# Neighbourhood attention with query blocks shifted by 8 columns and stacked hi/lo operands; the dilated second score over the full array

## Chip, cores and metric

One core of one Trainium2 chip runs the kernel. The metric is device time in microseconds of one execution, the median of the runs; lower is better.

## What is computed

A two-layer encoder over 512 positions of width 1024, batch 1, everything in float32. A layer mixes with 16 heads of 64 (4 differential, 6 dilated, 6 neighbourhood heads), projects the heads back, and applies a gated convolution MLP; both parts are modulated by vectors computed from `c`. What the change touches, cut from the reference:

```python
def neighborhood_attention(q, k, v, rpb):          # grid of 8 rows x 64 columns, position = 64 r + c
    # a query sees all 8 rows and the 16 columns from clip(c - 8, 0, 48)
    s = einsum('bhrqd,bhrjkd->bhrqjk', qg, kr) * (DH ** -0.5) + bias
    s = where(col_mask, s, NEG)
    p = softmax(s.reshape(B, H, rows, 64, 8 * 64))
    return einsum('bhrqn,bhrnd->bhrqd', p, vr)

def dilated_attention(q, k, v):                    # three dilated windows, merged by their log sums
    ...

o = concatenate([o_diff, o_dilated, o_neighbourhood]) @ w_out
x = x + gate * o
```

## The kernel before

**Number format.** A float32 product is made from `fp32r` matmuls: each operand is split into a rounded part (hi) and the rest (lo), and hi·hi, hi·lo and lo·hi are summed in PSUM (`mm3`, L482 to L485). Weights come as float32 from memory on SP's queue (`emit_raw`, L329), ScalarE rounds them (L351) and VectorE or GpSimd subtracts (L353); three or so units of weights are kept ahead.

**Phases.** For each of the two layers: `attention_phase` (projections, then heads), then `ffn_phase`, which begins with `o2`, the part of the output projection that reads the neighbourhood heads, `oT[5]` to `oT[7]`. `o1`, the part that reads the other five chunks, still belongs to `attention_phase`.

**Order of the work in `attention_phase`.** A generator `proj` walks through the projections: V of the differential and dilated heads, Q/K of the dilated pairs, Q/K of neighbourhood pairs 0 and 1 (`qk_na`), V of the neighbourhood heads (L761 to L771), Q/K of pair 2, and, once the dilated heads are done, the split of the first five chunks of the heads' output (L776 to L781) and `o1` (L782 to L788). Beside it runs the list `steps`: 16 differential steps, 24 dilated steps (6 heads x 4 query blocks of 128) and 12 neighbourhood steps (6 heads x 2). Each pass of the loop at L1068 emits about six projection matmuls and, if a step's credit, buffers and keys allow, one step. A step issues its scores at once and its later stages as a chain with lags counted in passes (`Clock.chain`, L278). The framework takes this program order as priority and may put a ready instruction ahead of one that waits. Buffers are counted by hand in `av` (`tmp`, `s`, `pt`, `o`, `ph`, `nat`). In layer 0, `ada_step` (L402) adds one VectorE pass of 1024 columns per modulation column every fourth pass of the loop.

**Dilated step** (`dil_step`, L931). `dil_stack` (L645) has put Khi over Klo on 128 partitions (`ks`) and Qhi twice (`qs`); one full matmul gives Qhi·(Khi + Klo) (L938). The second, L939, multiplies Qlo (tile `ql`) by Khi and uses 64 partitions, those of the head. A VectorE pass adds the mask and takes the extreme (L942), ScalarE takes the exponential and scales (L947, L952), PE transposes P (L813), ScalarE rounds it (L817), VectorE subtracts (L821), and `av_half` multiplies V (whose hi and lo columns stand side by side, so the output has 128 rows) by hi and lo of P (L834, L836). The two halves of the output are then added: a ScalarE copy (L844) and a VectorE addition (L847).

**Neighbourhood step** (`na_step`, L967). `qk_na` (L723) leaves hi and lo of Q and K in column-major order in four tiles `nat`, a head on 64 partitions. A step takes two blocks of 128 queries (16 columns x 8 rows), each with a window of 32 columns (256 keys): three matmuls of 64 partitions per block (L981 to L983). VectorE adds the bias and takes the maximum (L988), ScalarE the exponential (L998), VectorE normalises (L1004), PE transposes four tiles (L1010), ScalarE copies them (L1013), and four float32 products with V (L1027, which the chip runs as eight matmuls of 64 output rows) go into one PSUM tile for two heads. Per pair, ScalarE rounds it (L1035) and VectorE subtracts (L1036) into `oT`. The bias of a head is 384 KB and uses the `ks` buffers (`nab_load`, L962). V of these heads is written to DRAM (L767) and, when the dilated heads are done, loaded in seven windows (`v_na`, L790 to L795).

Of the kernel before, what the change touches and what calls it, by code (L numbers as in the profile page):

```python
# [144 lines left out]
WIN = (0, 8, 24, 32)  # L145


def _na_index():
    idx = np.full((3, 128, 256), -1, np.int64)
    for t, (b, w0) in enumerate(((0, 0), (1, 8), (3, 32))):  # L150
        for q in range(128):
            c, r = 16 * b + q // 8, q % 8
            cs = min(max(c - KW // 2, 0), GW - KW)
            for j in range(256):
                kc, kr = w0 + j // 8, j % 8
                if cs <= kc < cs + KW:
                    idx[t, q, j] = (kr - r + KH - 1) * (2 * KW - 1) + kc - c + KW - 1
    return idx
# [15 lines left out]
def build(ctx, tc, a):  # L174
# [393 lines left out]
    def attention_phase(l, gen, fest):  # L568
# [13 lines left out]
        scr, stk, vs, of, oT, nab, dns = {}, {}, {}, {}, {}, {}, {}  # L582
# [62 lines left out]
        def dil_stack(p):  # L645
# [3 lines left out]
            L = at([128, S], F32R, "ql", 2)  # L649
# [6 lines left out]
            SY.dma_start(Lf[0:64], sv[0, 64:128, 0])  # L656
            SY.dma_start(Lf[64:128], sv[0, 64:128, 1])
# [3 lines left out]
        def v_rows(name, nu, kper, n, done):  # L661
# [11 lines left out]
            for tb, k in seq:  # L673
# [9 lines left out]
                ts = slice(tb * 128, tb * 128 + 128)  # L683
                PE.matmul(outs[tb], h[k][0][:, ts], wh[:, sl], start=(k == 0), stop=False)
                PE.matmul(outs[tb], h[k][0][:, ts], wl[:, sl], start=False, stop=False)
                PE.matmul(outs[tb], h[k][1][:, ts], wh[:, sl], start=False, stop=(k == KD - 1))
# [36 lines left out]
        def qk_na(p):  # L723
            res = []
            for nm, scale in (("cq", 0.125), ("ck", 1.0)):
                b = yield from bank()
                yield from proj_cols((nm, p), h, b)
                while av["nat"] < 2:
                    yield
                av["nat"] -= 2  # L730
                hi = at([128, GW, GR], F32R, "nat", 8)
                lo = at([128, GW, GR], F32R, "nat", 8)
                bv = b.rearrange("p (r c) -> p r c", r=GR)
                hv, lv = hi.rearrange("p c r -> p r c"), lo.rearrange("p c r -> p r c")
                A.activation(out=hv, in_=bv, func=AF.Copy, scale=scale)

                def fin(lv=lv, bv=bv, hv=hv, scale=scale):
                    V.scalar_tensor_tensor(out=lv, in0=bv, scalar=scale, in1=hv.bitcast(F32),
                                           op0=ALU.mult, op1=ALU.subtract)
                    give("pr")  # L740

                ck.after(1, fin)
                res += [hi.rearrange("p c r -> p (c r)"), lo.rearrange("p c r -> p (c r)")]
            stk["c", p] = res
            mark(2, ("c", p))

        def proj():
# [13 lines left out]
            sv = dp.tile([GR, GW, HC * 64], F32, name=f"scv{l}")  # L761
            vt = at([128, 4, HC * 64], F32, "va", 1)

            def done(tb, src, ptag):
                A.copy(vt[:, tb], src)
                give(ptag)
                ck.after(1, lambda: SY.dma_start(sv[2 * tb:2 * tb + 2], vt[:, tb]))  # L767

            yield from v_rows("vc", 4, 2, 384, done)
            ready.add("sv")  # L770
            vs["sv"] = sv  # L771
# [4 lines left out]
            for c in range(5):  # L776
# [4 lines left out]
                oT[c] = (hi, lo)  # L781
            for m in range(KD):  # L782
# [6 lines left out]

        def v_na():  # L790
            vn = at([128, 7, HC * 64], F32, "vb", 1)
            for i in range(7):
                SY.dma_start(vn[:, i], vs["sv"][:, 8 * i:8 * i + 16].rearrange("r c n -> c r n"))
            vs["vc"] = vn
            mark(3, "vc")  # L795
# [32 lines left out]
        def av_half(st, half, vt, hidx, c, hh, fin):  # L828
# [9 lines left out]
            if half == 1:  # L838
                if c not in of:
                    of[c] = at([128, S], F32, "of", 5)  # L840
                t = tmp()
                dst = slice(64 * hh, 64 * hh + 64)
                oth = slice(64 - 64 * hh, 128 - 64 * hh)
                A.copy(t[dst], o[oth])  # L844

                def s1():
                    V.tensor_tensor(out=of[c][dst], in0=o[dst], in1=t[dst], op=ALU.add)  # L847
                    give("o")
                    if fin:
                        fin()  # L850

                ck.after(1, s1)
# [78 lines left out]
        def dil_step(hd, qb, st):  # L931
            p, hh = divmod(hd, 2)
            K, Q, L = stk["b", p]
            lr = slice(64 * hh, 64 * hh + 64)
# [4 lines left out]
            PE.matmul(s, L[lr, sl], K[lr, hh], start=False, stop=True)  # L939
# [22 lines left out]
        def nab_load(hd):  # L962
            b = at([128, 3, 256], F32, "ks", 2)
            SY.dma_start(b, a["nab"][l, hd])
            nab[hd] = b

        def na_step(hd, q2, st):  # L967
            p, hh = divmod(hd, 2)
            qh, ql, kh, kl = stk["c", p]
            hr = slice(64 * hh, 64 * hh + 64)  # L970
            bias = nab[hd]
            vn = vs["vc"]
# [3 lines left out]
            P = take("tmp", (128, 2, 256))  # L976
            for i in range(2):
                qb = 2 * q2 + i
                sl = slice(qb * 128, qb * 128 + 128)
                kw = slice(WIN[qb] * 8, WIN[qb] * 8 + 256)  # L980
# [3 lines left out]
            if hh == 1 and q2 == 1:  # L984
                av["nat"] += 4
            for i in range(2):
                bt = (0, 1, 1, 2)[2 * q2 + i]
                V.tensor_tensor_reduce(out=P[:, i], in0=s[:, i], in1=bias[:, bt], op0=ALU.add, op1=ALU.max,  # L988
                                       scale=1.0, scalar=-3e38, accum_out=mx[:, i:i + 1])
# [4 lines left out]
            box = {}  # L994

            def s1():
                for i in range(2):
                    A.activation(out=P[:, i], in_=P[:, i], func=AF.Exp, bias=mx[:, i:i + 1],  # L998
                                 accum_out=dn[:, i:i + 1])

            def s2():
                V.reciprocal(out=dn, in_=dn)
                for i in range(2):
                    V.tensor_scalar(out=P[:, i], in0=P[:, i], scalar1=dn[:, i:i + 1], scalar2=None, op0=ALU.mult)  # L1004

            def s3():
                pt = take("pt", (128, 2, 2, 128))
                for i in range(2):
                    for kt in range(2):
                        PE.transpose(pt[:, i, kt], P[:, i, kt * 128:kt * 128 + 128], ident)  # L1010
# [4 lines left out]
                box["p"] = ptn  # L1015

            def s4():
                ptn = box["p"]
                if hh == 0 and q2 == 0:
                    of["c", p] = take("o")  # L1020
                o = of["c", p]
                hs = slice(hd * 64, hd * 64 + 64)
                for i in range(2):
                    qb = 2 * q2 + i
                    w = WIN[qb] // 8
                    for kt in range(2):
# [308 lines left out]
```

## Time and profile before

| what | value |
|---|---|
| median of 3 runs | 1386.52 us (1386.37 to 1387.81) |
| profiled execution: span from first to last instruction | 1383.9 us |
| PE, VectorE, ScalarE busy | 1328.0, 896.2, 608.2 us |
| mean granted TensorE clock | 0.990 of 2.4 GHz |
| first layer's dilated scores on PE | 166.8 us on |
| first layer's neighbourhood scores on PE | 250.7 us on |
| last neighbourhood product of layer 1 | starts at 981.5 us |

The profile gives no time of the profiled execution outside its span; what lies around the span is taken as the difference to the median, 2.6 us. In its lines "PE" is TensorE's matmuls, "PEld" its weight loads, "DVE" VectorE, "ACT" ScalarE, "POOL" GpSimd and "SP" the engine whose queue issues most transfers. A matmul's duration contains its passage through the array, so that consecutive matmuls overlap; the cost of one in a stream is the distance between starts. A line of a group gives its count, then busy time in all and mean ns of one, then the idle time before them and what ended it.

### The profile page before, as it was taken

The page shows a single profiled execution, that of the slowest core. Times are in us where ns is not written, and L with a number is a line of the kernel's source. Part 1 is how long each engine was busy: PE and PEld are TensorE (multiplying, and loading weights), DVE is VectorE, ACT ScalarE, POOL GpSimd, SP SyncE. Part 2 cuts the span into 40 slices and gives each one's busy share as a digit, 9 for nine tenths or more (in the row PEclk, how much of TensorE's full clock was granted, in tenths as well). Part 3 has the DMA queues.
Part 4 walks back from the last instruction along what each step waited for, and adds up shares of the span by engine and source line. Part 5 has one row for each costly group of instructions (what it writes and reads, how often), then busy time and mean ns, then how long its engine had stood idle before and what let it go on. Part 6 is the DMA issues. An engine that isn't in the chain of part 4 may idle for free.

```text
span 1383.9 us, 18577 instructions
## 1 busy us (share of the span) xinstructions
PE 1328.0 (96%) x6992; PEld 1109.3 (80%) x6992; DVE 896.2 (65%) x1615; ACT 608.2 (44%) x1051; POOL 177.8 (13%) x116
## 2 busy tenths in 40 slices
PE   5887899999999999999998989999999999999997
PEld 4785678779988888888898867877898888888886
DVE  7968976977776666656675697466576434443443
ACT  3336487645543233223342667775445322332331
POOL 3732321003000000000113232200200000000002
PEclk9999999999999999999999999999999999999998
DMA  9565564644466666665523645142334323333211
GB/s 365 164 182 150 162 208 142 197 134 149 124 195 181 202 180 184 198 196 165 175 76 108 178 140 171 57 126 77 97 98 124 103 94 91 96 102 92 79 44 61
DMA packets 69262, 196.16 MB, mean 142 GB/s; under 512 B 7602, under 2 KB 12850, under 8 KB 69044
## 3 DMA queue, kind: packets, MB, share of 16 engines
q1 hardware_dynamic: 68448, 193.10, 46.3%
q10 hardware_dynamic: 724, 1.87, 0.4%
q8 instruction: 55, 0.90, 0.3%
q14 instruction: 35, 0.29, 0.1%
HBM read 180.78 MB, written 14.16 MB: 141 GB/s over the span
## 4 chain that ended last, share of the span: by engine, by line
PE 85%; DVE 8%; DMA 3%; POOL 2%; issue 1%; ACT 1%; POOLq 0%; SPq 0%; DVEq 0%; ACTq 0%
PE pr L483 12%; PE pr L485 12%; PE pr L484 11%; PE s L484 5%; PE s L485 5%; PE s L483 5%; PE pt L484 4%; PE pt L485 4%; PE pt L483 4%; PE pt L813 2%; PE o L485 2%; PE o L483 2%; PE o L484 2%; PE o L1027 2%; PE s L939 1%
## 5 line engine op out<-in xcount | busy, mean ns | idle before, releaser
L351 ACT CAST whi<-raw 128x1024 fp32r<-128x1024 f32 (+2 forms) x144 | 135.0, 938 | 268.8 <-PE pr L485 103.4
L353 DVE TENSOR_TENSOR wlo<-raw,whi 128x1024 fp32r<-128x1024 f32 (+2 forms) x101 | 111.2, 1101 | 94.9 <-ACT whi L351 94.1
L444 POOL TENSOR_TENSOR tmp<-tmp,tmp 128x256 f32<-128x256 f32 (+1 forms) x38 | 36.7, 966 | 892.5 <-ACT tmp L442 891.2
L351 ACT CAST fhi<-raw 128x1024 fp32r<-128x1024 f32 (+1 forms) x76 | 74.9, 985 | 143.9 <-PE pr L485 53.7
L411 DVE CUSTOM_DVE_ANT_0 tmp<-raw,cb,par 128x1024 bf16<-128x1024 f32 x80 | 106.8, 1336 | 41.6 <-DMA raw<-w_ada 41.5
L485 PE MATMUL pr<-h,whi 128*128 128x512 f32 (+1 forms) x330 | 121.9, 374 | 8.0 <-POOL h L479 7.6
L483 PE MATMUL pr<-h,whi 128*128 128x512 f32 (+1 forms) x330 | 125.9, 382 | 1.6 <-DVE tmp L596 0.7
L353 POOL TENSOR_TENSOR wlo<-raw,whi 128x768 fp32r<-128x768 f32 (+1 forms) x43 | 96.0, 2238 | 243.2 <-ACT whi L351 215.6
L484 PE MATMUL pr<-h,wlo 128*128 128x512 f32 (+1 forms) x330 | 123.1, 373 | 1.0 <-POOL wlo L353 1.0
L353 DVE TENSOR_TENSOR flo<-raw,fhi 128x1024 fp32r<-128x1024 f32 (+1 forms) x76 | 87.4, 1150 | 55.2 <-ACT fhi L351 54.4
L483 PE MATMUL pr<-h,fhi 128*128 128x512 f32 (+1 forms) x244 | 86.7, 357 | 0.0
L484 PE MATMUL pr<-h,flo 128*128 128x512 f32 (+1 forms) x244 | 86.5, 356 | 0.0
L485 PE MATMUL pr<-h,fhi 128*128 128x512 f32 (+1 forms) x244 | 85.5, 357 | 0.5 <-DVE h L479 0.5
L485 PEld LDWEIGHTS pr<-h,whi 128*128 128x128 f32 x330 | 62.1, 190 | 19.8 <-POOL h L479 9.5
L483 PEld LDWEIGHTS pr<-h,whi 128*128 128x128 f32 x330 | 62.7, 190 | 16.0 <-issue 4.1
L484 PEld LDWEIGHTS pr<-h,wlo 128*128 128x128 f32 x330 | 63.1, 191 | 9.7 <-POOL wlo L353 1.2
L1157 ACT ACTIVATE tmp<-tmp 128x512 f32<-128x512 f32 x44 | 27.6, 631 | 94.3 <-DVE tmp L1152 77.4
L821 DVE TENSOR_TENSOR pl<-pt,ph 128x512 fp32r<-128x512 f32 x80 | 54.4, 686 | 14.7 <-ACT ph L817 14.5
L904 DVE TENSOR_REDUCE sm<-s 128x1 f32<-128x512 f32 x64 | 43.0, 682 | 28.4 <-PE s L902 28.0
L813 PE MATMUL pt<-cst,tmp 128*128 128x128 f32 x320 | 48.6, 274 | 13.3 <-DVE tmp L920 11.0
L817 ACT CAST ph<-pt 128x512 fp32r<-128x512 f32 x80 | 46.7, 586 | 32.3 <-PE pt L813 31.2
L477 ACT ACTIVATE h<-tmp,mod,gsc 128x256 fp32r<-128x256 f32 (+1 forms) x58 | 35.3, 621 | 53.3 <-DVE tmp L474 52.5
(265 smaller groups left out, 3657.3 us busy)
## 6 DMA issues: line engine op xcount, KB each, us to landing
raw<-w SPq DMA_DIRECT2D x132, 512.0 KB
raw<-w_ada SPq DMA_DIRECT2D x80, 512.0 KB
raw<-w SPq DMA_DIRECT2D x72, 384.0 KB
araw<-w_ada SPq DMA_DIRECT2D x16, 512.0 KB
raw<-w SPq DMA_DIRECT2D x16, 320.0 KB
ks<-nab SPq DMA_DIRECT2D x12, 384.0 KB
scr0b<-nat SPq DMA_DIRECT2D x12, 256.0 KB
scr1b<-nat SPq DMA_DIRECT2D x12, 256.0 KB
```

What stands on the lines that cost most here:

```text
L351: A.copy(hi, r)
L353: (G if on_pool else V).tensor_tensor(out=lo, in0=r, in1=hi.bitcast(F32), op=ALU.subtract)
L411: V.tensor_tensor_reduce(out=junk, in0=r, in1=cb, op0=ALU.mult, op1=ALU.add, scale=1.0, scalar=par[:, OFF_B + l * 48 + j:OFF_B + l * 48 + ...
L444: self.last = self.eng.tensor_tensor(out=self.sq[0][:, sl], in0=self.sq[0][:, sl], in1=self.sq[m][:, sl], op=ALU.add)
L477: ins = A.activation(out=hi, in_=t, func=AF.Identity, scale=A_col, bias=sh_col)
L483: PE.matmul(out, wh, hh, start=first, stop=False)
L484: PE.matmul(out, wl, hh, start=False, stop=False)
L485: return PE.matmul(out, wh, hl, start=False, stop=last)
L813: PE.transpose(pt[:, kt], P[:, kt * 128:kt * 128 + 128], ident)
L817: A.copy(st["ph", half][:, :, sl], pt)
L821: V.tensor_tensor(out=st["pl", half][:, :, sl], in0=st["pt", qb], in1=st["ph", half][:, :, sl].bitcast(F32), op=ALU.subtract)
L904: V.tensor_reduce(out=nm[:, m:m + 1], in_=s, axis=AX.X, op=ALU.max, negate=True)
```

## The change

The dilated Qlo tile gets 128 rows, Qlo twice, for both heads; the second score becomes Qlo·(Khi + Klo) with 128 partitions. For the neighbourhood heads:

- queries are rotated by 8 columns, so that a block of 128 holds columns 16b - 8 to 16b + 7; the first block holds columns 56 to 63 and 0 to 7. Inner blocks see exactly two tiles of 16 columns (128 keys each), the two halves of the first block one tile each;
- hi and lo of Q and K are stacked on 128 partitions by 12 transfers a pair (`na_stack`), and two full matmuls replace three of 64 partitions;
- V is split into hi and lo, written to DRAM and loaded as four column tiles right after its projection; P is transposed to seven tiles a head, split into hi and lo, and ten `fp32r` matmuls a head give the product, whose halves are added as for the other heads;
- the bias of a head shrinks to 128 x 384 values (192 KB) with buffers of its own.

```diff
-            L = at([128, S], F32R, "ql", 2)
+            L = at([128, 2, S], F32R, "ql", 2)
-            SY.dma_start(Lf[0:64], sv[0, 64:128, 0])
-            SY.dma_start(Lf[64:128], sv[0, 64:128, 1])
+            SY.dma_start(Lf[0:64], sv[0, 64:128])
+            SY.dma_start(Lf[64:128], sv[0, 64:128])
...
+        def na_stack(p):
+            qh, ql, kh, kl = [t.bitcast(F32) for t in natc[p]]
...
+            for i in range(2):
+                rows = slice(64 * i, 64 * i + 64)
+                SY.dma_start(Kf[0:64, i], kh[rows])
+                SY.dma_start(Kf[64:128, i], kl[rows])
+                for half in range(2):
+                    SY.dma_start(Qf[64 * half:64 * half + 64, i], qh[rows])
+                    SY.dma_start(Lf[64 * half:64 * half + 64, i], ql[rows])
+            av["nat"] += 4
...
+            yield from v_rows("vc", 4, 2, 384, v_split("va", HC, "vt"))
...
+            for tb in range(4):
+                SY.dma_start(sv[2 * tb:2 * tb + 2], vt[:, tb])
+            vn = at([128, 4, HC, 128], F32R, "va", 1)
+            for t in range(4):
+                SY.dma_start(vn.bitcast(F32)[:, t].rearrange("p h d -> p (h d)"), sv[:, 16 * t:16 * t + 16])
...
-            PE.matmul(s, L[lr, sl], K[lr, hh], start=False, stop=True)
+            PE.matmul(s, L[:, hh, sl], K[:, hh], start=False, stop=True)
...
-                PE.matmul(s[:, i], qh[hr, sl], kh[hr, kw], start=True, stop=False)
-                PE.matmul(s[:, i], qh[hr, sl], kl[hr, kw], start=False, stop=False)
-                PE.matmul(s[:, i], ql[hr, sl], kh[hr, kw], start=False, stop=True)
+                PE.matmul(s[:, i], Q[:, hh, sl], keys, start=True, stop=False)
+                PE.matmul(s[:, i], L[:, hh, sl], keys, start=False, stop=True)
+            if q2:
+                work = [(slice(0, 128), i, s[:, i], bias[:, 128:384], slice(256 * i, 256 * i + 256)) for i in range(2)]
...
+            else:
+                work = [(slice(0, 64), 0, s[0:64, 0, 128:256], bias[0:64, 0:128], slice(0, 128)),
+                        (slice(64, 128), 0, s[64:128, 0, 0:128], bias[64:128, 0:128], slice(0, 128)),
+                        (slice(0, 128), 1, s[:, 1], bias[:, 128:384], slice(128, 384))]
...
+                pt = take("pt", (128, n, 128))
+                for i in range(n):
+                    PE.transpose(pt[:, i], P[:, i * 128:i * 128 + 128], ident)
                 give("tmp")
-                ptn = take("tmp", (128, 2, 2, 128))
-                A.copy(ptn, pt)
+                A.copy(st["ph"][:, at0:at0 + n], pt)
...
+                V.tensor_tensor(out=st["pl"][:, at0:at0 + n], in0=box["pt"],
+                                in1=st["ph"][:, at0:at0 + n].bitcast(F32), op=ALU.subtract)
...
+                todo = [(ph, t) for ph in ("ph", "pl") for t in ((0, 0, 192, 64), (1, 64, 320, 256),
+                                                                 (2, 192, 448, 512), (3, 320, 448, 768),
+                                                                 (3, 448, 512, 0))]
+                for i, (ph, (t, q0, q1, c0)) in enumerate(todo):
+                    PE.matmul(o[:, q0:q1], vn[:, t, hd, :],
+                              st[ph].rearrange("p a b -> p (a b)")[:, c0:c0 + q1 - q0],
+                              start=(i == 0), stop=(i == len(todo) - 1), skip_group_check=True)
+                give("ph")
+                halves(o, 5 + p, hh, (lambda: na_out(p)) if hh == 1 else None)
...
+            if q2:
+                chain.append((2, {"o": 1, "if": lambda: "oT" in ready}, s5))
...
+        for p, at_step in enumerate((NDB - 8, NDB, NDB + 4)):
+            stacks.append((("natc", p), at_step, lambda p=p: na_stack(p)))
```

`halves` holds the copy and the addition that `av_half` had (L841 to L852). `na_out` rounds and subtracts per pair as L1035 and L1036 did, from the added tile. `"oT"` becomes ready after the split of the first five chunks. NDB is 40, the number of differential and dilated steps, so the stacks are issued from step 32, 40 and 44 on. `qk_na` writes K in natural order (one contiguous ScalarE and VectorE instruction each) and Q in two pieces.

## Rows read from the trace of the kernel before

**Rows 1.** The page, busy time of the engines: busy us (share of the span) xinstructions.

```profile
PE 1328.0 (96%) x6992; PEld 1109.3 (80%) x6992; DVE 896.2 (65%) x1615; ACT 608.2 (44%) x1051; POOL 177.8 (13%) x116
```

**Rows 2.** Busy time by stretch, with granted clock, DMA share and GB/s.

```profile
core 0: us, PE busy (x) PEld busy (x) DVE busy (x) ACT busy (x) POOL busy (x), PEclk, DMA share, GB/s
174.00:248.00 74.00, 74.00 (x394) 58.36 (x393) 51.98 (x125) 59.07 (x112) 13.82 (x7) 1.00 0.54 165
840.00:914.00 74.00, 74.00 (x395) 59.02 (x393) 41.59 (x100) 57.30 (x109) 14.89 (x8) 1.00 0.36 105
248.00:322.70 74.70, 74.70 (x426) 58.92 (x426) 59.70 (x167) 39.97 (x92) 0.00 (x0) 1.00 0.58 179
914.00:990.80 76.80, 76.80 (x427) 59.59 (x428) 47.66 (x138) 41.87 (x94) 0.00 (x0) 1.00 0.33 98
```

**Rows 3.** The chain of waits, layer 0: start us, us, what.

```profile
197.47 0.43 PE s L939
...
296.34 1.02 PE o L1027 x8
```

**Rows 4.** Timeline of PE around a dilated score, layer 1: start us, us, instruction.

```profile
911.03 0.39 PE L485 MATMUL pr<-h,whi 128*128 128x512 f32 x1
911.26 0.40 PE L938 MATMUL s<-ks,qs 128*128 128x512 f32 x1
911.59 0.49 PE L939 MATMUL s<-ks,ql 64*128 64x512 f32 x1
912.01 0.50 PE L483 MATMUL pr<-h,whi 128*128 128x512 f32 x1
912.35 0.39 PE L484 MATMUL pr<-h,wlo 128*128 128x512 f32 x1
```

**Rows 5.** Timeline of PE, one neighbourhood step in o1, layer 1.

```profile
946.21 0.38 PE L981 MATMUL s<-nat,nat 64*128 64x256 f32 x1
...
947.10 0.50 PE L483 MATMUL pr<-oh,whi 128*128 128x512 f32 x1
...
949.37 1.09 PE L1027 MATMUL o<-tmp,vb 128*64 128x128 f32 x8
950.39 0.66 PE L1010 MATMUL pt<-cst,tmp 128*128 128x128 f32 x4
950.98 0.38 PE L981 MATMUL s<-nat,nat 64*128 64x256 f32 x1
```

**Rows 6.** Timeline of PE, a dilated product and the transposes behind it, layer 1.

```profile
905.36 0.64 PE L834 MATMUL o<-ph,vb 128*128 128x256 f32 x4
905.83 0.64 PE L836 MATMUL o<-pl,vb 128*128 128x256 f32 x4
906.31 0.60 PE L813 MATMUL pt<-cst,tmp 128*128 128x128 f32 x4
906.67 0.48 PE L938 MATMUL s<-ks,qs 128*128 128x512 f32 x1
```

**Rows 7.** Groups of VectorE by shape, whole span: count, busy us, mean ns, idle before.

```profile
L821 DVE TENSOR_TENSOR pl<-pt,ph 128x512 fp32r<-128x512 f32 x80 | 54.4, 686 | 14.7 <-ACT ph L817 14.5
L988 DVE CUSTOM_DVE_ANT_0 tmp<-s,ks 128x256 f32<-128x256 f32 x48 | 18.9, 424 | 6.1 <-PE s L983 6.0
L847 DVE TENSOR_TENSOR of<-o,tmp 64x512 f32<-64x512 f32 x20 | 13.7, 686 | 7.7 <-ACT tmp L844 7.4
L707 DVE TENSOR_TENSOR vb<-pr,vb 128x384 fp32r<-128x384 f32 x6 | 3.3, 545 | 0.0
```

**Rows 8.** Waits of SP's queue, whole span: us in total, times, longest us.

```profile
SPq L964 <- PE s L939: 21.0, 4, 8.5
```

**Rows 9.** Timeline of SP's queue, layer 0: start us, us, issues.

```profile
257.20 4.42 SPq L793 DMA_DIRECT2D vb<-scv  x7
262.75 0.33 SPq L964 DMA_DIRECT2D ks<-nab  x1
```

**Rows 10.** Timeline of PE, last product and first o2 matmul, layer 1.

```profile
981.51 1.09 PE L1027 MATMUL o<-tmp,vb 128*64 128x128 f32 x8
...
990.82 0.28 PE L483 MATMUL pr<-oh,whi 128*128 128x256 f32 x1
```

More of the change, by code (lines that the diff above doesn't have):

```diff
@@ L142, in _consts, with _na_block @@
     return cst, np.ascontiguousarray(rope.astype(np.float32).transpose(1, 0, 2))
-WIN = (0, 8, 24, 32)
-def _na_index():
[L149 to L158, printed above, removed]
+def _na_block(c0, tiles):
+    idx = np.full((64, 128 * len(tiles)), -1, np.int64)
+    for q in range(64):
+        c, r = c0 + q // 8, q % 8
+        cs = min(max(c - KW // 2, 0), GW - KW)
+        for j in range(idx.shape[1]):
+            kr, kc = j % 128 // 16, 16 * tiles[j // 128] + j % 16
+            if cs <= kc < cs + KW:
+                idx[q, j] = (kr - r + KH - 1) * (2 * KW - 1) + kc - c + KW - 1
+    return idx
+def _na_index():
+    edge = np.concatenate([_na_block(56, (3,)), _na_block(0, (0,))])
+    mid = [np.concatenate([_na_block(16 * b + 8, (b, b + 1)), _na_block(16 * b + 16, (b, b + 1))]) for b in range(3)]
+    assert (mid[0] == mid[1]).all() and (mid[0] == mid[2]).all()
+    return np.concatenate([edge, mid[0]], axis=1)
 CST, ROPE = _consts()
@@ L682, in v_rows @@
                 sl = slice(j * n, j * n + n)
[L683 to L686, printed above, removed]
+                hh, hl = [t[:, tb * 128:tb * 128 + 128] for t in h[k]]
+                PE.matmul(outs[tb], hh, wh[:, sl], start=(k == 0), stop=False)
+                PE.matmul(outs[tb], hh, wl[:, sl], start=False, stop=False)
+                PE.matmul(outs[tb], hl, wh[:, sl], start=False, stop=(k == KD - 1))
                 if k == KD - 1:
@@ L730, in qk_na @@
                 av["nat"] -= 2
[L731 to L739, printed above, removed]
+                hi = at([128, S], F32R, "nat", 8)
@@ L760, in proj @@
                 yield
[L761 to L771, printed above, removed]
+            yield from v_rows("vc", 4, 2, 384, v_split("va", HC, "vt"))
+            sv = dp.tile([GR, GW, HC * 128], F32, name=f"scv{l}")
+            vt = vs["vt"].bitcast(F32).rearrange("p a h d -> p a (h d)")
+            for tb in range(4):
[3 more added lines that the diff above has]
+                SY.dma_start(vn.bitcast(F32)[:, t].rearrange("p h d -> p (h d)"), sv[:, 16 * t:16 * t + 16])
+            vs["vc"] = vn
+            mark(3, "vc")
             yield from qk_na(2)
@@ L838, in av_half, with halves, s1 @@
             if half == 1:
[L839 to L852, printed above, removed]
+                halves(o, c, hh, fin)
+        def halves(o, c, hh, fin):
+            if c not in of:
+                of[c] = at([128, S], F32, "of", 5)
+            t = tmp()
+            dst = slice(64 * hh, 64 * hh + 64)
+            oth = slice(64 - 64 * hh, 128 - 64 * hh)
+            A.copy(t[dst], o[oth])
+            def s1():
+                V.tensor_tensor(out=of[c][dst], in0=o[dst], in1=t[dst], op=ALU.add)
+                give("o")
+                if fin:
+                    fin()
+            ck.after(1, s1)
         def diff_norm(c):
@@ L1003, in s2 @@
                 for i in range(2):
-                    V.tensor_scalar(out=P[:, i], in0=P[:, i], scalar1=dn[:, i:i + 1], scalar2=None, op0=ALU.mult)
+                    V.tensor_scalar(out=P[:, cols[i]], in0=P[:, cols[i]], scalar1=dn[:, i:i + 1], scalar2=None,
+                                    op0=ALU.mult)
             def s3():
[L1007 to L1010, printed above, removed]
@@ L1011, in s3 @@
-                give("tmp")
-                ptn = take("tmp", (128, 2, 2, 128))
-                A.copy(ptn, pt)
-                give("pt")
[L1015 to L1026, printed above, removed]
-                        PE.matmul(o[hr, qb * 128:qb * 128 + 128], vn[:, w + 2 * kt, hs], ptn[:, i, kt],
-                                  start=(kt == 0), stop=(kt == 1))
-                give("tmp")
-                if hh == 1 and q2 == 1:
-                    hi = wp.tile([128, S], F32R, tag="h", bufs=16, name=f"oh{uid()}")
-                    lo = wp.tile([128, S], F32R, tag="h", bufs=16, name=f"ol{uid()}")
-                    ov = o.rearrange("p (c r) -> p r c", r=GR)
-                    hv, lv = hi.rearrange("p (r c) -> p r c", r=GR), lo.rearrange("p (r c) -> p r c", r=GR)
-                    A.copy(hv, ov)
-                    V.tensor_tensor(out=lv, in0=ov, in1=hv.bitcast(F32), op=ALU.subtract)
-                    give("o")
-                    oT[5 + p] = (hi, lo)
```

99 lines of the change are left out of this document (64 added, 35 removed).

## The prediction, made before the changed kernel was built or run

> **What bounds the kernel now.** I read the page first: TensorE (PE) is busy nearly the whole span [rows 1], but that is an average, so I cut out the four stretches which the change touches and asked for busy time of every engine in each [rows 2]: the dilated steps of the two layers (74.0 us each) and what follows them up to the first o2 matmul, with all neighbourhood steps (74.7 and 76.8 us). PE never idles in any of them at full clock; in the first two ScalarE is next (59.1 and 57.3 us), in the last two VectorE (59.7 and 47.7 us). VectorE is fuller in layer 0, where it also computes the adaLN modulation. The chain of waits confirms it: from about 172 us its links are PE's own instructions, the second dilated score (0.43 us a link) and later the fp32 products with V (1.02 us) [rows 3]. A PE microsecond taken out there shortens the path until VectorE or ScalarE ends later. Busy time hides the pitch (instructions overlap), so every PE price below is a difference of two start times in the timeline.
>
> **Dilated second score.** An undisturbed 128x512 matmul starts 0.23 us after the one before (911.03 to 911.26) [rows 4]. Around the dilated pair the steps are 0.33 (L938 to L939), 0.42 (L939 to the next) and 0.34 (that one to the one after). From 911.03 to 912.35 are four intervals, 1.32 us, against 4 x 0.23 = 0.92: the 64-row matmul costs its neighbours 0.40 us, although it streams the same 512 columns as L938. With L and K of 128 rows it is the form that L938 has, so I take all 0.40 as saved: 48 x 0.40 = 19.2 us of PE, 9.6 a layer. Bounds: 0 (if the excess belonged to another operand and not to the 64 rows) and 19.2.
> The Trainium skill's TensorEngine Tiling (Key Properties) says that changing the tiling mode drains the engine, which would give these 0.40 us. Its TensorE: Matmul & The Clock Gate (Why this matters for your kernels) says that a matmul of few contraction rows takes the same time as one of 128; read alone, that makes this term 0 and speaks against the change. The 0.33, 0.42 and 0.34 side with the first; the second is rival B.
>
> **Neighbourhood step on PE.** One step's period in layer 1 is 946.21 to 950.98, 4.77 us, and holds nine o1 matmuls from 947.10 on [rows 5]; less 9 x 0.23 = 2.07 the step costs 2.70 us, of which 0.89 are six half-array scores, 1.02 the fp32 products with V, 0.59 four transposes and the switch behind them, the rest the switches in the o1 run. After: four full-array scores of 256 columns. Four such matmuls start within 0.47 us in the dilated product (905.36 to 905.83), and four transposes take 0.36 [rows 6]. So scores 0.48; 3.5 transposes (three in one step, four in the other) 0.32, plus 0.09 for the change of form behind them; five of the head's ten products with V, 960 columns, between 0.45 (by columns) and 0.60 (by count), I take 0.55, nearer the count since two of ten are as short as 64 columns. Sum 1.44, saved 1.26, times 24 steps: 30 us of PE, 15 a layer. Bounds: 0.85 a step if each of four changes of operand costs another 0.10 (20 us), 1.36 if products go by columns (33 us). With the dilated term PE sheds 49 us, between 20 (0 + 20) and 52 (19 + 33).
>
> **What VectorE takes over.** Each head now splits P into hi and lo: one subtraction of 512 columns, 0.69 us, and one of 384, between 0.52 and 0.69, taken 0.6 [rows 7]; the two product halves are added, 0.69; the edge block is reduced in two pieces of 64 rows, one instruction more per head, between 0 and 0.42, taken 0.2 as it has half the columns. 2.2 us a head, 13 a layer, in the neighbourhood stretch. Stretch of layer 0: VectorE 59.7 + 13 = 72.7, PE 74.7 - 15 = 59.7. VectorE becomes the bound and only 2 us are gained. Layer 1: VectorE 60.7, PE 61.8. Two engines in order that feed each other don't both run full; I take halfway between 61.8 and the present 76.8, a gain of 7.5 us. Nothing lets VectorE shed the modulation work of layer 0, which the next phase needs.
> The dilated stretch: the V rows of the last group now get a lo part, 4 x 0.55 = 2.2 us of VectorE [rows 7]; PE goes to 64.4, ScalarE stays at 59.1 and 57.3 (92% and 89% of it), VectorE in layer 0 at 54. Still PE's, but close; I keep three quarters of 9.6, 7.2 a layer.
>
> **Moved and added at no cost.** Three stacks a layer, each 12 transfers of 128 KB on SP's queue, wait for the matmul that last read the buffer. Today's waits of that kind were at most 8.5 us [rows 8]; seven V loads were issued in 4.42 us, 0.63 each, against 0.33 for a bias load [rows 9]: 4 to 7.6 us of issue a stack. What hides it: each stack is issued at least four steps (4 x (4.77 - 1.26) = 14 us) before its first reader, and the weight loads queued behind it are three units ahead of use, 3 x 24 x 0.23 = 16.6 us. Cover gone, PE waits for weights; priced in rival D. The V loads move in front of the last dilated steps, so the first products no longer follow a load; SP waits there for four stores, within the same 16.6 us. The bias gets its own buffers and half the bytes, so the four waits of its loads on L939 [rows 8] go and the stacks' waits take their place. The split of cq becomes two instructions and that of ck turns contiguous; I set them even. ScalarE gets one 64x512 copy a head, about the length of the VectorE addition behind it, under 5 us in a stretch where it has over 30 free.
> At the end of the stretch the product now passes one copy and one addition more before o2. The last product starts at 981.51 and o2 at 990.82 [rows 10]; 9.3 us cover one addition of 0.69 us [rows 7] and a copy of about that length. The new condition that products wait for the first five oT splits only changes the order: o1 fills PE meanwhile.
>
> **Sum.** 2 x 7.2 + 2 + 7.5 = 24 us of gain. The profiled span is 1383.9 us; the median run, 1386.5, lies 2.6 above it, which I carry over: 1359.9 + 2.6 = 1362.5, say **1362**.
>
> **Rivals.**
> A: VectorE does not bind, because its new work slips into the idle time of the dilated stretch and of the o2 stage and the modulation is passed by. Then PE's 49 us come whole or nearly: 41 to 52 gained, 1334 to 1345. For: PE idles nowhere now. Against: 72.7 in a stretch that PE would leave at 59.7. Chance 0.10.
> B: only streamed columns count, half-array or not. Dilated gain 0; of the step 2 x 0.12 of scores, 0.47 of products and 0.04 of transposes remain, 0.75 x 24 = 18 us of PE, of which VectorE leaves 2 in layer 0 and 8 in layer 1: about 10 gained, 1376. For: the same column count. Against: the three long intervals. A tight VectorE and ScalarE in both stretches end in the same place. 4 to 16 gained, chance 0.17.
> C: gain and new waits cancel, within 0.2% (2.8 us, about what a measurement of this kernel tells from no change): 0.05.
> D, slower: SP's queue. A stack holds the weight loads behind it for its wait plus its issue, 8.5 + 7.6 = 16.1 us at the worst of today's rows, and decides from 16.6 on. Six stacks must each stop PE by more than 24 / 6 = 4 us to eat the gain; at 8 us each the time is 1362 + 48 = 1410. For: the stacks wait for the newest matmul of the program. Against: no wait of 20 us stands in today's rows, and the dilated stacks queue in the same way. Chance 0.08.
> Forecast: 17 to 40 gained, 1346 to 1369, chance 0.60.
>
> **Numbers.** Range 1342 to 1380: the forecast's cases, B, and a part of A; beyond lie most of D and C and the best of A, about 0.2. Faster 0.87 (forecast, A, B), same 0.05, slower 0.08.
>
> **What would show it.** Right: intervals of 0.23 around both dilated scores; four scores, one transposing group and ten products at 1.4 to 1.5 us a step; the second stretch of layer 0 limited by VectorE above 90% busy with PE idle behind it, and less so in layer 1; dilated stretches shorter by 7 to 10 us. Wrong: a second score that still takes 0.42 (B); PE without idle time in layer 0's neighbourhood stretch (A); PE waiting for split weights right after a stack's issue (D); or the other stretches, which I leave alone, moving by more than 3 us.

## The result and the profile after

The changed kernel takes **1367.57 us** (median of 4 runs, 1365.54 to 1370.58), the kernel before 1387.11 us beside it: ratio 0.9864, interval [0.9852, 0.9877], 19 us gained where 24 were forecast. The time lies in the range and in the forecast's own case, but the sum reached it by two errors of opposite sign: layer 1 gained more than I said, and layer 0's neighbourhood part, which should have gained 2 us, lost about 7.

The profiled execution took 1369.17 us, its span is 1367.4 us. The page's busy times stand against [rows 1]:

```profile
PE 1290.9 (94%) x6860; PEld 1101.6 (81%) x6860; DVE 918.2 (67%) x1689; ACT 607.3 (44%) x1069; POOL 178.1 (13%) x116
```

PE's sum of overlapping instructions fell by 37 us, VectorE's rose by 22, and the time fell by 19, about half of what PE shed. To see where the rest went, I cut each layer behind the dilated steps at three marks: the start of the last dilated score, of the first o2 matmul, and of the first ScalarE instruction of the MLP's convolution. The first stretch holds the neighbourhood steps, the second o2 and what leads into the MLP. Busy time by stretch, kernel before (columns as in [rows 2]; layer 0, then layer 1):

```profile
247.00:322.70 75.70, 75.70 (x429) 59.38 (x428) 59.87 (x167) 40.83 (x95) 0.00 (x0) 1.00 0.58 176
322.70:372.10 49.40, 49.13 (x413) 48.78 (x412) 35.00 (x74) 24.80 (x41) 11.99 (x13) 1.00 0.37 112
913.50:990.80 77.30, 77.30 (x429) 59.78 (x428) 47.66 (x138) 42.29 (x96) 0.00 (x0) 1.00 0.33 98
990.80:1040.10 49.30, 49.04 (x414) 48.81 (x413) 33.56 (x73) 24.30 (x41) 11.45 (x13) 1.00 0.36 107
```

The same stretches of the changed kernel:

```profile
241.00:310.40 69.40, 62.96 (x357) 52.37 (x356) 61.99 (x183) 40.48 (x98) 0.00 (x0) 0.98 0.68 188
310.40:373.30 62.90, 54.81 (x419) 53.20 (x419) 44.37 (x90) 27.73 (x46) 11.54 (x13) 0.95 0.43 133
908.80:973.70 64.90, 62.38 (x364) 53.03 (x363) 56.14 (x167) 43.07 (x101) 0.00 (x0) 1.00 0.51 134
973.70:1023.90 50.20, 49.35 (x414) 48.90 (x413) 35.66 (x76) 25.86 (x44) 11.11 (x13) 1.00 0.37 113
```

Layer 1 is what one hopes for: the neighbourhood stretch is 12.4 us shorter, PE is still busy in 62.4 of 64.9 us, and the o2 stretch stays. Layer 0 gains 6.3 us in the first stretch and **loses 13.5 in the second**, in which the change leaves the work of o2 as it was. There PE idles 8 us, its clock is lower, and VectorE has 9.4 us more to do. The dilated steps, from the first score to the last, went from 80.2 to 73.5 us in layer 0 and from 80.9 to 73.4 in layer 1.

**The dilated pair.** Timeline of PE, changed kernel, layer 0, against [rows 4]:

```profile
238.89 0.39 PE L488 MATMUL pr<-h,whi 128*128 128x512 f32 x1
239.12 0.39 PE L960 MATMUL s<-ks,qs 128*128 128x512 f32 x1
239.35 0.40 PE L961 MATMUL s<-ks,ql 128*128 128x512 f32 x1
239.58 0.39 PE L486 MATMUL pr<-h,whi 128*128 128x512 f32 x1
239.82 0.40 PE L487 MATMUL pr<-h,wlo 128*128 128x512 f32 x1
```

All four intervals are 0.23 or 0.24: the whole 0.40 us a pair is gone, though the second score streams as many columns as before. This answers rival B. The Trainium skill's TensorEngine Tiling (Key Properties), by which a change of the tiling mode drains the engine, agrees with the trace here: the 0.40 us came with the 64-row score and went with it. Its TensorE: Matmul & The Clock Gate (Why this matters for your kernels) says that a single matmul of few rows takes the time of a full one; no run here has such a matmul by itself, and in this stream the next matmul started 0.42 us after the 64-row one and starts 0.23 after the full one.

**The neighbourhood step.** Timeline of PE, changed kernel, two steps among o1 matmuls of layer 1, against [rows 5]:

```profile
936.44 0.49 PE L1041 MATMUL pt<-cst,tmp 128*128 128x128 f32 x3
936.69 0.36 PE L1002 MATMUL s<-ks,qs 128*128 128x256 f32 x1
936.89 0.28 PE L1003 MATMUL s<-ks,ql 128*128 128x256 f32 x1
937.01 0.28 PE L1002 MATMUL s<-ks,qs 128*128 128x256 f32 x1
937.13 0.28 PE L1003 MATMUL s<-ks,ql 128*128 128x256 f32 x1
937.25 0.39 PE L486 MATMUL pr<-oh,whi 128*128 128x512 f32 x1
...
937.95 0.65 PE L1058 MATMUL o<-ph,va 128*128 128x192 f32 x5
938.43 0.80 PE L1058 MATMUL o<-pl,va 128*128 128x192 f32 x5
939.07 0.48 PE L486 MATMUL pr<-oh,whi 128*128 128x512 f32 x1
939.38 0.40 PE L487 MATMUL pr<-oh,wlo 128*128 128x512 f32 x1
...
940.53 0.60 PE L1041 MATMUL pt<-cst,tmp 128*128 128x128 f32 x4
940.88 0.37 PE L1002 MATMUL s<-ks,qs 128*128 128x256 f32 x1
...
941.45 0.40 PE L486 MATMUL pr<-oh,whi 128*128 128x512 f32 x1
```

Transposes and scores take 0.81 us in the step with three tiles (936.44 to 937.25) and 0.92 in the one with four (940.53 to 941.45). A head's ten products take 1.12 (937.95 to 939.07) and the matmul behind them 0.08 more than 0.23, so 0.60 for each of its two steps. The mean is 0.87 + 0.60 = 1.47 us, forecast 1.44.

**VectorE's new work.** Groups of VectorE by shape, changed kernel, against [rows 7]:

```profile
L870 DVE TENSOR_TENSOR of<-o,tmp 64x512 f32<-64x512 f32 x32 | 21.9, 685 | 3.1 <-ACT tmp L867 2.6
L1013 DVE CUSTOM_DVE_ANT_0 tmp<-s,nab 128x256 f32<-128x256 f32 x36 | 14.4, 417 | 0.2
L1047 DVE TENSOR_TENSOR pl<-pt,ph 128x512 fp32r<-128x512 f32 x12 | 8.2, 682 | 0.7 <-ACT ph L1043 0.7
L1013 DVE CUSTOM_DVE_ANT_0 tmp<-s,nab 64x128 f32<-64x128 f32 x24 | 6.9, 286 | 1.5 <-DMA nab<-nab 1.4
L1047 DVE TENSOR_TENSOR pl<-pt,ph 128x384 fp32r<-128x384 f32 x12 | 6.6, 550 | 0.1
```

A head pays 0.68 + 0.55 for the subtractions, 0.69 for the addition of the halves (12 more than before) and (14.4 + 6.9 - 18.9) / 12 = 0.2 for the edge block: 2.1 us, forecast 2.2.

**Where layer 0 loses it.** Timeline of the changed kernel in layer 0, SP's queue and PE around the second stack:

```profile
257.17 0.59 SPq L769 DMA_DIRECT2D ql<-nat  x1
259.36 0.40 PE L488 MATMUL pr<-ol,whi 128*128 128x512 f32 x1
264.06 0.36 PE L1002 MATMUL s<-ks,qs 128*128 128x256 f32 x1 [4.30 <-issue]
...
265.42 0.63 PE L488 MATMUL pr<-ol,whi 128*128 128x512 f32 x1
265.85 0.63 PE L486 MATMUL pr<-oh,whi 128*128 128x512 f32 x1
```

This stack's last transfer is issued at 257.17, and its first score waits until 264.06; the matmuls behind start 0.43 us apart instead of 0.23. And in the o2 stretch, VectorE's modulation passes (L414), the loads that feed them (L402) and the weight loads behind those (L332) beside five of PE's waits:

```profile
310.31 7.49 SPq L402 DMA_DIRECT2D raw<-w_ada  x4
311.66 1.28 DVE L414 CUSTOM_DVE_ANT_0 tmp<-raw,cb,par 128x1024 bf16<-128x1024 f32 x1
312.87 0.49 PE L486 MATMUL pr<-oh,whi 128*128 128x512 f32 x1 [0.81 <-ACT oh L1075]
315.28 1.28 DVE L414 CUSTOM_DVE_ANT_0 tmp<-raw,cb,par 128x1024 bf16<-128x1024 f32 x1 [1.19 <-DMA raw<-w_ada]
317.50 0.38 PE L487 MATMUL s<-oh,flo 128*128 128x256 f32 x1 [2.04 <-DVE flo L356]
318.23 1.28 DVE L414 CUSTOM_DVE_ANT_0 tmp<-raw,cb,par 128x1024 bf16<-128x1024 f32 x1
318.34 8.64 SPq L332 DMA_DIRECT2D raw<-w  x5
320.28 1.28 DVE L414 CUSTOM_DVE_ANT_0 tmp<-raw,cb,par 128x1024 bf16<-128x1024 f32 x1
320.35 0.39 PE L486 MATMUL pr<-oh,whi 128*128 128x256 f32 x1 [0.70 <-DVE x L1134]
322.29 0.39 PE L486 MATMUL pr<-oh,whi 128*128 128x256 f32 x1 [0.60 <-DVE x L1134]
329.67 1.01 PE L456 MATMUL pt<-cst,tmp 128*128 128x1 f32 x4 [3.05 <-POOL tmp L447]
```

Before, all twelve passes of these two stretches ran in the first one; now eight do, and four lie beyond the first o2 matmul (311.66 to 320.28), where the split of the MLP's weights (flo) and the additions to x (L1134) stand behind them on VectorE. They are there by the program's order: followed through the two kernels' code, the loop that deals out a modulation pass every fourth round makes 124 rounds before and 112 after, since the neighbourhood steps begin in round 81 instead of 90 (they no longer wait for V to be loaded behind the dilated heads). One of the four belongs to the last round, and three are left for the end of the phase (`while ada_st["n"] < 40`). They are 5.1 of the 9.4 us that VectorE has more; 1.9 are the addition and the split for the last heads, which now come late, and most of the rest are splits of MLP weights. The loads of modulation columns and of weights share SP's queue and its four `raw` buffers, and a buffer with a column is free only when VectorE has made its pass.

### The profile page after: what moved, and what is told of

It is laid out like the page before. It is cut to its first block, busy times and chain, and to the rows that moved or that the text cites. A ratio compares the mean times of both kernels' runs of the same rounds, so it can differ in the third digit from the quotient of the medians.

```text
span 1367.4 us, 18510 instructions
## 1 busy us (share of the span) xinstructions
PE 1290.9 (94%) x6860; PEld 1101.6 (81%) x6860; DVE 918.2 (67%) x1689; ACT 607.3 (44%) x1069; POOL 178.1 (13%) x116
## 4 chain that ended last, share of the span: by engine, by line
PE 72%; DVE 14%; DMA 5%; ACT 3%; issue 3%; POOL 2%; SPq 0%; POOLq 0%; DVEq 0%; ACTq 0%
PE pr L488 10%; PE pr L487 9%; PE pr L486 9%; PE s L487 5%; PE s L486 5%; PE s L488 5%; PE pt L488 4%; PE pt L487 4%; PE pt L486 4%; PE o L487 2%; PE o L486 2%; PE o L488 2%; PE pt L833 2%; DMA raw<-w 2%; DVE tmp L414 2%
## 5 line engine op out<-in xcount | busy, mean ns | idle before, releaser
L447 POOL TENSOR_TENSOR tmp<-tmp,tmp 128x256 f32<-128x256 f32 (+1 forms) x38 | 36.6, 966 | 881.4 <-ACT tmp L445 880.4
L414 DVE CUSTOM_DVE_ANT_0 tmp<-raw,cb,par 128x1024 bf16<-128x1024 f32 x80 | 108.5, 1356 | 51.2 <-DMA raw<-w_ada 50.6
L487 PEld LDWEIGHTS pr<-h,wlo 128*128 128x128 f32 x330 | 62.9, 191 | 10.5 <-POOL wlo L356 1.7
L841 DVE TENSOR_TENSOR pl<-pt,ph 128x512 fp32r<-128x512 f32 x80 | 54.2, 683 | 11.9 <-ACT ph L837 11.7
```

The costliest lines, as they stand in the source:

```text
L414: V.tensor_tensor_reduce(out=junk, in0=r, in1=cb, op0=ALU.mult, op1=ALU.add, scale=1.0, scalar=par[:, OFF_B + l * 48 + j:OFF_B + l * 48 + ...
L447: self.last = self.eng.tensor_tensor(out=self.sq[0][:, sl], in0=self.sq[0][:, sl], in1=self.sq[m][:, sl], op=ALU.add)
L487: PE.matmul(out, wl, hh, start=False, stop=False)
L841: V.tensor_tensor(out=st["pl", half][:, :, sl], in0=st["pt", qb], in1=st["ph", half][:, :, sl].bitcast(F32), op=ALU.subtract)
```

## Experiments

All times are medians of 4 to 6 runs; ratios are to the kernel before on the same chip (1386.0 to 1387.3 us in the three series). Differences in the text are between medians, partly from different chips; by the ratios they come out within 2 us of these. The table, to which the texts below refer, has the two stretches of layer 0 from one profile of each kernel, from the last dilated score to the first o2 matmul and from there to the MLP's first convolution. The profile of e8 is that of the slowest of its four runs, 1359.93 us.

| kernel | us | ratio, interval | neighbourhood, layer 0 | o2, layer 0 |
|---|---|---|---|---|
| before | 1386.52 | | 75.7 | 49.4 |
| dilated part alone (e1) | 1370.58 | 0.9884 [0.9867, 0.9900] | 75.4 | 49.6 |
| neighbourhood part alone (e2) | 1381.86 | 0.9963 [0.9949, 0.9977] | 66.6 | 64.2 |
| changed | 1367.57 | 0.9864 [0.9852, 0.9877] | 69.4 | 62.9 |
| neighbourhood part in layer 1 only (e6) | 1360.08 | 0.9811 [0.9797, 0.9826] | 75.4 | 49.3 |
| changed, no loads (e7) | 1354.35 | 0.9769 [0.9754, 0.9783] | 63.6 | 60.2 |
| changed, short passes (e8) | 1355.18 | 0.9761 [0.9736, 0.9786] | 69.5 | 52.8 |
| changed, neither (e11) | 1344.64 | 0.9695 [0.9681, 0.9710] | 64.5 | 52.3 |
| dilated alone, no loads (e9) | 1364.42 | 0.9842 [0.9827, 0.9857] | 75.3 | 49.4 |
| dilated alone, short passes (e10) | 1371.61 | 0.9889 [0.9873, 0.9906] | 77.0 | 49.9 |
| dilated alone, neither (e12) | 1364.03 | 0.9832 [0.9818, 0.9847] | 77.1 | 49.3 |
| changed, one stack of three (e5) | 1361.56 | 0.9819 [0.9791, 0.9847] | 64.8 | 62.7 |
| changed, o1 split on GpSimd (e3) | 1370.18 | 0.9877 [0.9861, 0.9894] | 73.0 | 58.8 |
| changed, modulation every third pass (e4) | 1372.72 | 0.9903 [0.9885, 0.9920] | 72.0 | 58.3 |

### The two parts by themselves

e1 is the kernel before with the diff's lines of the dilated part (the tile, its two transfers, the second score; cut below), e2 the changed kernel with them put back:

```diff
-            L = at([128, S], F32R, "ql", 2)
+            L = at([128, 2, S], F32R, "ql", 2)
...
-            PE.matmul(s, L[lr, sl], K[lr, hh], start=False, stop=True)
+            PE.matmul(s, L[:, hh, sl], K[:, hh], start=False, stop=True)
```

> The kernel before with the dilated second score over 128 partitions and nothing else of the change. Theory (a 64-row matmul between full ones costs its neighbours 0.40 us, and PE sets the pace of the dilated stretches): the intervals around both scores become 0.23 us and the time falls by 12 to 19 us, to 1368 to 1375. Rival (only streamed columns count): the time stays within 2 us of 1387.

> The changed kernel with the dilated second score put back to 64 partitions. If layer 0 is held by VectorE and by what follows it, the dilated gain is lost there anyway and shows in layer 1 alone: 5 to 8 us above the changed kernel, 1373 to 1376. If the two parts add up, 12 to 19 us above it, 1380 to 1387. If only columns count, the same as the changed kernel, 1366 to 1370.

The dilated part alone gains 0.0116 x 1386.5 = 16 us, forecast 14.4. The neighbourhood part gains 5 alone, and some 3 on top of the dilated part (1370.58 to 1367.57). The parts add up within about 2 us, which is the second case of e2's expectation, so the small gain of the neighbourhood part belongs to itself and not to a collision of the two.

The change also sets `dynamic_dma_scratch_size=4096` where the kernel is created. All kernels of the table but the first have it, so no run shows its effect by itself. There is little room for one: in e1 the dilated steps are shorter by 6.0 and 7.2 us (74.2 and 73.7 us), which makes up the 13.0 us between the two profiled spans (1383.9 to 1370.9), and the two stretches behind them stay as they were.

### The neighbourhood part in one layer

e6 has in layer 0 the attention phase of before with the dilated part (`attention_phase0`), and that of the changed kernel in layer 1 (with the old bias as a second table):

```diff
-        oT = attention_phase(l, rb0, fest)
+        oT = (attention_phase0 if l == 0 else attention_phase)(l, rb0, fest)
```

> The dilated part in both layers, the neighbourhood part in layer 1 alone (layer 0 keeps the neighbourhood code of before). Measured so far from the profiles: in layer 0 the neighbourhood part costs about 6 us up to the first convolution of the MLP, in layer 1 it gains 10 to 11. If these are effects of the layers themselves, this kernel takes 1358 to 1363 us, 5 to 9 less than the changed kernel. If the sign came from the order that the framework happened to find, it lies anywhere from 1364 to 1372.

Measured 1360.08 us. From e1 to e6 the neighbourhood part is added in layer 1: a gain of 10.5 us. From e6 to the changed kernel it is added in layer 0 too: **a loss of 7.5 us**. This is also the fastest kernel of the study that computes everything, 0.9811 [0.9797, 0.9826] of the time before and 7.5 us better than the change as it was made.

### What layer 0 has that layer 1 has not: loads and passes of the modulation

e7 and e9 leave out 24 of the loads of modulation columns (the passes run at full width, with `cb` itself in the place of the loaded column), e8 and e10 leave the loads and cut 24 of the passes from 1024 to 64 columns, e11 and e12 do both:

```diff
+        if 16 <= i < 40:
+            ada_raw.append(cb)
+            return
...
+        w = 64 if 16 < ada_st["n"] <= 40 else D
-        V.tensor_tensor_reduce(out=junk, in0=r, in1=cb, ...
+        V.tensor_tensor_reduce(out=junk[:, 0:w], in0=r[:, 0:w], in1=cb[:, 0:w], ...
```

> The changed kernel without the 24 modulation loads (512 KB each) of layer 0's attention phase: the VectorE pass stays and reads the tile of c twice, so columns 16 to 39 of layer 0's modulation are wrong. If the loads hold layer 0 (they share four buffers and SP's queue with the weights, and VectorE alone frees theirs): 8 to 17 us less than the changed kernel, 1350 to 1360. If VectorE's busy time holds it: 1364 to 1369.

> The changed kernel with those 24 loads kept and the VectorE pass over them cut to 64 of 1024 columns (28 us of VectorE less; columns 16 to 39 of layer 0's modulation are sums over 64 of c's 1024 entries). If VectorE's busy time holds layer 0: 8 to 17 us less than the changed kernel, 1350 to 1360. If the loads do: at most 4 us less, 1363 to 1368.

> The kernel with the dilated part alone, without the same 24 loads (same columns wrong): the base for the run without loads. If the loads are what turns the neighbourhood part's sign in layer 0, they cost little here (1366 to 1371), and the difference to the changed kernel without loads is 15 us or more, 8 to 11 of it in layer 0. If not, the difference stays near 4 us.

> The kernel with the dilated part alone, the 24 modulation passes of layer 0 cut to 64 of 1024 columns, loads kept (columns 16 to 39 of layer 0's modulation are sums over 64 entries): the base for the run with short passes (1355 us). The first convolution of layer 0 came at 362.8 us there. If VectorE's load alone turns the neighbourhood part's sign in layer 0, it comes at 372 to 375 here and the time is 1370 to 1376; if the loads do as well, at 360 to 366, and the time is 1364 to 1369.

> The changed kernel with neither the 24 loads nor their long passes (64 columns of the tile of c in their place, columns 16 to 39 of layer 0's modulation wrong): layer 0 is then loaded like layer 1. If modulation is all that sets the layers apart, the neighbourhood part gains 9 to 14 us in layer 0 against the next run but one here without modulation, and the time is 1340 to 1349. If something else holds layer 0 (the stack transfers), the time stays near 1354, that of the run without loads.

> The kernel with the dilated part alone and neither loads nor long passes: the base for the run of the changed kernel without modulation. PE sets the pace there already (PE busy 70.0 of 70 us between 240 and 310 us without loads), so both theories expect little against the run without loads alone: 1360 to 1365.

What the neighbourhood part is worth on top of the dilated part, from these medians: 3 us with loads and passes; 10 without the loads (1364.42 to 1354.35); 16 with short passes (1371.61 to 1355.18); 19 with neither (1364.03 to 1344.64). So each takes a share, and the gain lost to both is 16 us. The 10 us without loads lie between the two cases of e9's expectation (15 or more, near 4), and e10 met its first case in time (1371.61 us) but not in its mark: the first convolution came at 366.6 us, not at 372 to 375. The cut pass is the sharper probe: it is worth nothing to the dilated part alone (1370.58 to 1371.61) and 12 us to the changed kernel, so VectorE had room for its modulation work as long as PE took 75 us for the neighbourhood stretch.

The stretches tell which does what. Without the loads (e7), the two stretches of layer 0:

```profile
236.20:299.80 63.60, 61.78 (x357) 51.33 (x356) 61.60 (x183) 40.66 (x99) 0.00 (x0) 1.00 0.50 132
299.80:360.00 60.20, 53.24 (x420) 51.76 (x419) 43.79 (x90) 28.15 (x47) 11.62 (x13) 0.97 0.33 99
```

With short passes (e8):

```profile
240.50:310.00 69.50, 63.90 (x364) 54.12 (x363) 58.51 (x190) 42.83 (x101) 0.00 (x0) 0.98 0.70 202
310.00:362.80 52.80, 51.17 (x414) 50.47 (x413) 37.99 (x84) 25.38 (x43) 11.15 (x13) 0.97 0.42 131
```

With neither (e11):

```profile
233.30:297.80 64.50, 61.80 (x364) 53.01 (x363) 58.72 (x197) 43.11 (x101) 0.00 (x0) 1.00 0.51 137
297.80:350.10 52.30, 50.74 (x413) 50.30 (x412) 35.86 (x77) 25.53 (x43) 11.71 (x13) 0.97 0.35 105
```

All three leave the neighbourhood steps as they are. The loads lengthen the **first** stretch: 69.4 and 69.5 us where they run, 63.6 and 64.5 where they don't, with a DMA share of 0.68 to 0.70 against 0.50. The passes lengthen the **second**: 62.9 and 60.2 where they are whole, 52.8 and 52.3 where they are cut, with VectorE at 44 us against 36 to 38. That is about 5 and 9 us. A short pass also frees its `raw` buffer sooner, but e7 and e11 read `cb` and hold no such buffer, and the second stretch still falls from 60.2 to 52.3 us: that part is VectorE's time alone. With both, the two stretches of layer 0 take 132.3 us together; with neither, 116.8, and layer 1 of the changed kernel takes 115.1: these two things are nearly all that tells the layers apart.

VectorE is not what holds the first stretch. Without loads it is busy 61.6 of 63.6 us (97%), but so is PE (61.8), and with VectorE down to 58.7 (e11) the stretch stays at 64.5. With loads VectorE is at 89% and PE at 91%; taking 3.5 us from VectorE (e8) leaves 69.5 us, and taking away transfers shortens it (e7, and e5 below).

### The stacks

e5 issues the first of the three stacks of a layer and lets the other two pairs read it, which leaves out two thirds of the stacks' transfers:

```diff
+            if p:
+                av["nat"] += 4
+                stk["c", p] = stk["c", 0]
+                mark(2, ("c", p))
+                return
```

> The changed kernel with the stack of pair 0 used for all three pairs, so that 24 of 36 stack transfers of 128 KB a layer and their waits are left out (heads 2 to 5 of the neighbourhood group are computed from the Q and K of heads 0 and 1). If the transfers and the 4.3 us for which PE stood before the second pair's first score cost what was assumed to be hidden: 5 to 10 us less than the changed kernel, 1358 to 1363. If layer 0 is held by VectorE and the modulation loads in any case: 1365 to 1369.

6 us gained, though the four runs spread from 1358.1 to 1367.6 us; the first stretch of layer 0 has 4.6 of it (69.4 to 64.8), about as much as the loads give. PE's wait of 4.30 us at 264.06 is not in this profile, nor in those of e7 and e11; with short passes and all loads (e8) there is one of 2.77 us at the same place. So in these runs the wait came only with both, the stacks and the modulation's loads beside the weights; taking either away was enough. A kernel without both was not run.

### Two attempts to relieve VectorE

e3 gives the lo part of the o1 weights to GpSimd; e4 makes a modulation pass in every third pass of the loop instead of every fourth, so that more lie in the dilated stretch:

```diff
-        on_pool = (l == 0 and 0 < u < 8) or kind in ("b", "cq", "ck", "vc", "vb")
+        on_pool = (l == 0 and 0 < u < 8) or kind in ("b", "cq", "ck", "vc", "vb", "o1")
...
-            if l == 0 and nst % 4 == 0 and si >= 10 and ada_st["n"] < 40:
+            if l == 0 and nst % 3 == 0 and si >= 10 and ada_st["n"] < 40:
```

> The changed kernel, with the eight weight splits of o1 in each layer (0.83 us each on VectorE, 6.6 us a layer) moved to GpSimd, which is idle there. If VectorE holds the neighbourhood stretch: 4 to 10 us faster than the changed kernel, 1358 to 1364, most of it in layer 0. If the stack transfers or the modulation loads hold it: 1366 to 1370.

> The changed kernel, with the modulation pass of layer 0 emitted every third pass of the loop in place of every fourth, so that none is left for the end of the phase (four lie between 311 and 322 us now, with the weight loads queued behind them). If that tail holds the start of the MLP in layer 0: 3 to 10 us faster than the changed kernel, 1358 to 1365. If VectorE's load alone decides, moving it earlier changes less than 2 us either way.

Neither helped. e3, which fell on the side of its expectation where VectorE does not hold the neighbourhood stretch, shortens the o2 stretch by 4 us and lengthens the one before it by as much. e4, 5 us slower than the changed kernel and in neither case of its expectation, leaves no pass behind the first o2 matmul, and that stretch falls by 4.6 us to 58.3, but the dilated steps of layer 0 take 79.7 us instead of 73.5: the price of the passes and their loads seems to have moved there, which no further run tests. That the o2 stretch stays 6 us above e11's without a single pass in it was not followed further; a wait of 3.06 us for GpSimd's L447, as at 329.67 above, is half of it. A third set of buffers for the stacks, and stacks issued earlier, were not tried.

## Why the prediction was right, and where not

- **Dilated score: right.** 0.40 us a pair is gone in full. Of 9.6 us a layer I kept three quarters, 14.4 in all; 16 were measured.
- **Neighbourhood step on PE: right.** 1.47 us a step against 1.44; 24 x (2.70 - 1.47) = 29.5 us of PE removed, forecast 30. Five of the ten products with V have 896 columns and not the 960 that I counted; their 0.60 us is the bound by count, and I took 0.55.
- **VectorE's new work: right by the head** (2.1 us against 2.2). Its whole busy time rose by 22.0 us; 13 + 2.2 a layer would be 30. The rest are small savings elsewhere, among them the split of Q and K in longer pieces, that I had set even.
- **Layer 1: too cautious.** "I take halfway between 61.8 and the present 76.8" gave 7.5 us. The stretch came down to 64.9, and 10.5 us were gained (e1 to e6). VectorE was taken at 60.7 us there and measured 56.1, PE at 61.8 and measured 62.4. The two came within about 3 us of the fuller one's time; here, with the second engine 10% below the first, halfway was too much.
- **Layer 0: the step that failed** is "VectorE becomes the bound and only 2 us are gained". The comparison of busy times (72.7 against 59.7) was made inside the one stretch, and "nothing lets VectorE shed the modulation work" took that work to stay in it. The program's own order took a third of it out: the loop ran out 12 rounds early, and four passes moved past the first o2 matmul. VectorE was busy 62.0 us of that stretch's 69.4 and did not bind it; transfers held it above the 63.6 to 64.8 us that it takes without the loads or with one stack. The o2 stretch, which was costed at nothing, lost 13.5 us. It showed in my own mark for a wrong prediction, a stretch left alone that moves by more than 3 us.
- **The stacks' cover: wrong in layer 0.** "Each stack is issued at least four steps" before its first reader holds in the program's order, not in time. In the trace the second stack's issue begins at 242.80, goes on to 257.76 because of waits, for buffers that dilated scores still read and for transfers of V, and the first score starts 6.3 us after that, in a stretch with a DMA share of 0.90 (255 to 270 us). The waits themselves were no longer than forecast. Waits of SP's queue, changed kernel:

```profile
SPq L768 <- PE s L961: 6.6, 2, 4.2
SPq L765 <- DMA va<-scv: 5.1, 2, 3.3
```

- **Rival D had the place and not the mechanism.** The queue did cost: some 6 us without the stacks (e5). PE stood for the stack itself, though, not for weights behind it, and for 4.30 us at one place in place of six. **Rival A** was right that VectorE does not bind the neighbourhood stretch and that modulation passes end up in the o2 stage, but not that this is free: the short passes give the changed kernel 12 us, and 19 us were gained, not 41 to 52. **Rival B** is refuted by the intervals of 0.23 us.

The sum, forecast and measured: dilated 14.4 and 16; layer 1 7.5 and 10.5; layer 0 a gain of 2 and a loss of 7.5. That is 24 against 19. The errors of +1.6, +3 and -9.5 add up to -5.

## What to carry to other kernels

Background work that is dealt out by a count, here one pass in four rounds of a loop, is no fixed load of a stretch: when the change leaves the loop fewer rounds, the rest falls into the next stretch, and the price is read there. Dealing it out earlier (e4) did not save it: the earlier stretch became longer. So count the rounds again, cost a stretch together with the ones beside it, and list for each queue, VectorE's and SP's, what else has to pass through in the shorter time: here the modulation's loads and passes, hidden for 75 us, cost 16 us once PE needed 62. When two layers run the same code beside different background work, measure the change in each by itself; the best version may have it in one only.

## What the hardware showed beyond that

Two waits of PE cost more than their length here. After the 4.30 us at 264.06 consecutive 512-column matmuls started 0.43 us apart, which is the level of 1.2 GHz, where 0.23 is that of 2.4. The rows by stretch of the changed kernel show it:

```profile
255.00:270.00 15.00, 10.70 (x53) 8.74 (x52) 9.77 (x35) 4.93 (x15) 0.00 (x0) 0.89 0.90 231
330.00:345.00 15.00, 14.10 (x95) 13.82 (x95) 10.03 (x23) 5.21 (x10) 5.23 (x7) 0.79 0.28 89
```

By an estimate from these means, the first row's 15 us hold 0.11 x 15 = 1.7 us of lost clock. The second row follows the wait of 3.05 us at 329.67 and loses 0.21 x 15 = 3.2 us, as much as the wait. In layer 1, where PE never waits over 0.9 us in these stretches, the granted clock is 1.00 throughout. In the o2 stretch of layer 0 PE's idle time is 62.9 - 54.8 = 8.1 us, and the clock of 0.95 adds some 0.05 x 62.9 = 3.1 (an estimate too): together about 11 of the 13.5 us lost there.
